# A two-layer mixer kernel with its transposed operands laid block by block

## The chip, the cores and the metric

One core of one Trainium2 chip runs the whole program. The metric is the time of one execution in device microseconds (us); the kernel before was timed three times, and the median counts. The engines are TensorE (PE, with its weight loads PEld), VectorE (DVE), ScalarE (ACT), GpSimd (POOL) and SyncE (SP), which in this kernel issues the DMAs, one after the other from one queue.

## The reference

The input is one sequence of 2048 rows of 1024 numbers in float32. Two layers follow each other. Each layer multiplies its rows by a wide matrix, gives the columns to several mixers, and multiplies the joined results by a second matrix:

```
h = rms_norm(x) ; proj = h @ w_in            # 1024 -> 4652 columns
y = five mixers on the columns of proj       # gating, attention with forgetting, mLSTM, RWKV-7, memory
x1 = x + (y * silu(z)) @ w_out               # 1280 -> 1024
h2 = x1 @ w_in_2                             # 1024 -> 3272 columns
o  = sparse attention (top 256 keys per row) and HGRN-2 on the columns of h2
out = layer_norm(2**0.25 * x1 + o @ w_o_2)   # 1024 -> 1024
```

All of it has to come out with the precision of float32.

## The kernel before

The rows are cut into 16 blocks of 128. Every product with a matrix needs the rows transposed: 128 numbers of the inner dimension on the partitions. A block of 128 rows and 1024 columns is eight such tiles of 128 x 128. For precision each number is split into a high and a low part of type fp32r, and a product is three matmuls (high x high, high x low, low x high), lines 313 to 315 in `mm3`.

The transposed, split rows live in "slots". `split_tiles` makes one tile `slot` of 2 x `k.slot` numbers on each partition, and gives it the shape (part, tile a, row t): first all of the high part, then all of the low part, and in each, for each of the eight tiles a, the rows of all the blocks of that slot one after the other. A slot holds two or three blocks of eight tiles (`k.slot` is 3072 or 2048). So one block in it is 16 pieces of 128 numbers, 512 bytes each, on every partition. Two or three slots are in turn.

A slot is filled in two ways. `put_slots` with `put_T` transposes a block on PE into PSUM, writes the high part with ACT (line 269) and the low part with DVE (line 270), four tiles at a time; where the block is needed again, it stores it with one DMA of 1 MB in DRAM (line 248), in the tensor `xT` (11 blocks of the first layer) or `X1T` (16 blocks of the second). There a block's 16 pieces follow each other: 8 KB in a row for each partition. `get_slots` brings a block back with one DMA of 1 MB (line 255): 11 loads from `xT`, and 32 from `X1T`, where each block is used twice. That makes 27 stores and 43 loads, 70 transfers.

Two functions use slots. In `product_steps` (by way of `project_tm`) a block's tile is the stationary operand and the matrix streams; in the trace such a product reads `pj<-whi,slot`, the moving operand first. In `project_cm` the matrix is stationary and the rows of all two or three blocks of a slot stream at once, 256 or 384 columns: `pj<-slot,whi`. The matrices come by `load_w`: raw pieces (`wraw`, line 297) that ACT and POOL split (lines 300, 301), or, where they were put aside before, both parts ready from DRAM (line 284), 1 to 1.25 MB with 8 to 10 KB in a row on each partition.

The program runs in stages: the first layer's projections with RWKV and the forgetting attention between them (to some 1000 us), its other mixers and projections (to 1700 us), the output product and the second layer's first projections with the choice of keys (`dsa_pick`, to 2490 us and beyond), the second projections for HGRN (`proj2_chunk(..., "hgrn")`, chunks of 6, 6 and 4 blocks, 2493 to 3070 us), the gates (`gates`, 3070 to 3190 us) and the attention with the final product. A planner puts each engine's instructions in order when the program is built; loads of slots and of matrices are asked for early (`high_priority`). SP's queue runs in order, too: a transfer that has to wait holds all the later ones.

Of the kernel before, what the change touches and what calls it, by code (L numbers as in the profile page):

```python
# [9 lines left out]
F32 = mybir.dt.float32  # L10
F32R = mybir.dt.float32r
# [4 lines left out]
ALU = mybir.AluOpType  # L16
# [68 lines left out]
def bc(ap, n=128):  # L85

    return bass.AP(tensor=ap.tensor, offset=ap.offset, ap=[[0, n]] + [list(x) for x in ap.ap])
# [124 lines left out]
def rep(ap, d):  # L212

    s = list(ap.shape)
    return ap.unsqueeze(len(s)).to_broadcast(s + [d])
# [4 lines left out]

def split_tiles(k, nk=8):

    slot = k.big.tile([128, 2, k.slot], F32R, tag="slot", name="slot")
    n = k.slot // nk // 128 * 128
    return slot[:, :, 0:nk * n].rearrange("p q (a t) -> p q a t", a=nk)


def make_slots(k, fill, blocks, nk=8):

    per = k.slot // nk // 128  # L230
    per = -(-len(blocks) // -(-len(blocks) // per))
    slots = []
    for i, b in enumerate(blocks):
        if i % per == 0:
            v = split_tiles(k, nk)
            slots.append((v[:, 0], v[:, 1], min(per, len(blocks) - i)))
        with k.tc.high_priority(k.ahead):
            c = 128 * (i % per)
            fill(v[:, :, :, c:c + 128], b)
    return slots  # L240


def put_slots(k, rows, blocks, nk=8, keep=None):

    def fill(v, b):
        put_T(k, v[:, 0], v[:, 1], 0, rows(b), nk)
        if keep is not None:
            k.nc.sync.dma_start(out=keep[b], in_=v.rearrange("p q a t -> p (q a) t").bitcast(F32))
    return make_slots(k, fill, blocks, nk)


def get_slots(k, kept, blocks):

    def fill(v, b):
        k.nc.sync.dma_start(out=v.rearrange("p q a t -> p (q a) t").bitcast(F32), in_=kept[b])
    return make_slots(k, fill, blocks)


def put_T(k, hi, lo, col, rows, nk):

    nc = k.nc
    for g in range(0, nk, 4):
        n = min(4, nk - g)
        p = k.bank("tp", k.ptp)
        for j in range(n):
            k.transpose(p[:, 128 * j:128 * j + 128], rows[:, (g + j) * 128:(g + j) * 128 + 128])
        pv = p.rearrange("p (a t) -> p a t", a=4)[:, 0:n]
        h = hi[:, g:g + n, col:col + 128]
        nc.scalar.activation(out=h, in_=pv, func=ACT.Copy)
        nc.vector.tensor_tensor(out=lo[:, g:g + n, col:col + 128], in0=pv, in1=h.bitcast(F32), op=ALU.subtract)  # L270


def load_w(k, w, c0, c1, nk, more=(), keep=None):
# [35 lines left out]
def mm3(k, out, pairs, n):  # L309

    m = len(pairs)
    for i, (ah, al, bh, bl) in enumerate(pairs):
        k.nc.tensor.matmul(out=out, lhsT=ah, rhs=bh, start=(i == 0), stop=False)  # L313
        k.nc.tensor.matmul(out=out, lhsT=ah, rhs=bl, start=False, stop=False)  # L314
        k.nc.tensor.matmul(out=out, lhsT=al, rhs=bh, start=False, stop=(i == m - 1))  # L315


def project_steps(k, slots, w, c0, c1, nk, use, more=(), keep=None):

    yield from product_steps(k, slots, *load_w(k, w, c0, c1, nk, more, keep), use)  # L320


def product_steps(k, slots, wh, wl, use):

    nk, n = wh.shape[1:]
    b = 0
    for hi, lo, nb in slots:
        for j in range(nb):
            p = k.bank(k.pj_tag, k.pj)
            t = slice(128 * j, 128 * j + 128)  # L330
            mm3(k, p[:, 0:n], [(hi[:, a, t], lo[:, a, t], wh[:, a, 0:n], wl[:, a, 0:n]) for a in range(nk)], n)
            use(b, p[:, 0:n])
            b += 1
            yield
# [7 lines left out]
def project_cm(k, slots, w, c0, c1, nk, use, more=(), keep=None):  # L342

    wh, wl = load_w(k, w, c0, c1, nk, more, keep)
    for c in range(0, c1 - c0 + sum(b - a for a, b in more), 128):
        m = slice(c, c + 128)
        b = 0
        for hi, lo, nb in slots:
            p = k.bank(k.pj_tag, k.pj)
            t = slice(0, 128 * nb)  # L350
            mm3(k, p[:, t], [(wh[:, a, m], wl[:, a, m], hi[:, a, t], lo[:, a, t]) for a in range(nk)], 128 * nb)
            use(c // 128, b, p[:, t])
            b += nb


def norm_rows(k, x, g, b):

    nc = k.nc
    xt = k.wk.tile([128, D], F32, tag="xt", name="xt", bufs=2)
    nc.sync.dma_start(out=xt, in_=x)  # L360
    sq = k.wk.tile([128, D], BF16, tag="xs", name="xsq", bufs=1)
    ss = k.sm.tile([128, 1], F32, tag="xss", name="xss")
    nc.scalar.activation(out=sq, in_=xt, func=ACT.Square, accum_out=ss)
    nc.vector.tensor_scalar(out=ss, in0=ss, scalar1=1.0 / D, scalar2=EPS, op0=ALU.mult, op1=ALU.add)
    r = k.sm.tile([128, 1], F32, tag="xr", name="xr")
    k.rsqrt(r, ss, "x")
    nc.vector.scalar_tensor_tensor(out=xt, in0=xt, scalar=r[:, 0:1], in1=g, op0=ALU.mult, op1=ALU.mult)
    return xt
# [163 lines left out]
def mem_setup(k, mem, mem_norm_g, w_kv, k_g):  # L532

    nc = k.nc
    g = k.wk.tile([128, D], F32, tag="xt", name="mg")
    nc.sync.dma_start(out=g, in_=bc(mem_norm_g))
    v = split_tiles(k)
    hi, lo = v[:, 0], v[:, 1]
    for b in range(2):
        put_T(k, hi, lo, 128 * b, norm_rows(k, mem[b * 128:b * 128 + 128, :], g, b), 8)  # L540
    k.mem_d = k.dr.tile([64, 4, 256], F32, name="mem_kd"), k.dr.tile([128, 2, 256], F32, name="mem_vd")
    gcol = col2(k, "mgk", k_g, 1.0)
    for c in (0, 256):
        wh, wl = load_w(k, w_kv, c, c + 256, 8)
        for b in range(2):
            t = slice(128 * b, 128 * b + 128)
            p = k.bank("pj", k.pj)
            mm3(k, p[:, 0:256], [(hi[:, a, t], lo[:, a, t], wh[:, a, 0:256], wl[:, a, 0:256]) for a in range(8)], 256)
            x = k.wk.tile([128, WMAX], F32, tag="po", name="mkv", bufs=3)[:, 0:256]
            k.evict(x, p[:, 0:256])  # L550
            if c:
                nc.sync.dma_start(out=k.mem_d[1][:, b], in_=x)
                continue
            hx = x.rearrange("p (h d) -> p h d", d=64)
            sq = k.wk.tile([128, 256], F32, tag="zt", name="msq").rearrange("p (h d) -> p h d", d=64)
            r = k.head_rms(hx, 4, 64, "x", sq=sq)
            nc.vector.tensor_tensor(out=hx, in0=hx, in1=rep(r, 64), op=ALU.mult)
            p = k.bank("tp", k.ptp)
            for h in range(4):
                k.transpose(p[0:64, 128 * h:128 * h + 128], x[:, 64 * h:64 * h + 64])  # L560
            for i in range(2):
                o = k.wk.tile([128, 384], F32, tag="pq", name="mko")[0:64, 0:256]
                nc.vector.tensor_scalar(out=o, in0=p[0:64, 256 * i:256 * i + 256], scalar1=gcol[:, 0:1], scalar2=None,
                                        op0=ALU.mult)
                nc.sync.dma_start(out=k.mem_d[0][:, 2 * i:2 * i + 2, t], in_=o.rearrange("p (h t) -> p h t", h=2))
# [15 lines left out]
def col2(k, name, g, scale):  # L581

    c = k.const.tile([64, 1], F32, name=name)
    k.nc.sync.dma_start(out=c, in_=g.rearrange("(p o) -> p o", o=1))
    if scale != 1.0:
        k.nc.vector.tensor_scalar(out=c, in0=c, scalar1=scale, scalar2=None, op0=ALU.mult)
    return c
# [851 lines left out]
def gates(k, S, slots, wh, wl, blocks):  # L1439

    def use(b, p):
        o = k.wk.tile([128, 392], F32, tag="pg", name="pg")
        silu2(k, o, p, 392)
        k.nc.sync.dma_start(out=S["ga"][128 * blocks[b]:128 * blocks[b] + 128, 120:512], in_=o)

    for _ in product_steps(k, slots, wh, wl, use):
        pass
# [72 lines left out]
def final_attention(k, hold, g, w_o, ln_g, ln_b, out):  # L1520
    w = [load_w(k, w_o[0:512], c, c + 512, 4) for c in (0, 512)]
    for b, x in hold.items():
        v = split_tiles(k, 4)
        hi, lo = v[:, 0], v[:, 1]
        put_T(k, hi, lo, 0, g[b], 4)
        for c, (wh, wl) in zip((0, 512), w):
            p = k.bank("pj", k.pj)
            mm3(k, p, [(hi[:, a, 0:128], lo[:, a, 0:128], wh[:, a], wl[:, a]) for a in range(4)], 512)
            k.nc.vector.tensor_tensor(out=x[:, c:c + 512], in0=x[:, c:c + 512], in1=p, op=ALU.add)
        final_norm(k, x, ln_g, ln_b, out, b)  # L1530

# [776 lines left out]
```

## Time and profile before

| | |
|---|---|
| Median of three runs | 3763.75 us (3760.35 to 3767.74) |
| The profiled execution | 3754.19 us, of which the span of the trace is 3752.3 us |
| Busy: PE / DVE / ACT / POOL | 3521.8 / 2430.2 / 1393.1 / 624.0 us |
| Mean granted clock of PE | 0.962 |
| DMA | 692 MB, mean 185 GB/s |

Busy time is the time in which an engine has an instruction under way. "Idle before" is the time for which the engine stood still ahead of an instruction, with what released it. The granted clock is a share of full speed; 1.00 is TensorE at 2.4 GHz, 0.50 at 1.2 GHz. On the SP queue the length of a DMA row is the time that the issue took, not the transfer; "us to landing" is the time from the issue until the data is there. A row with x2 or more joins several issues that follow each other, with what lay between them.

### The profile page before, as it was taken

How to read it: one execution, taken by the hardware profiler on the slowest of the kernel's cores; microseconds unless marked ns; L12 is line 12 of the kernel's file. 1: busy time of each engine (PE TensorE's matmuls, PEld its weight loads, DVE VectorE, ACT ScalarE, POOL GpSimd, SP SyncE). 2: the span in 40 equal slices, each digit the busy share in tenths (PEclk: the TensorE clock that was granted, in tenths of full speed). 3: DMA queues.
4: the chain of work that ended last, by engine and by line, in shares of the span. 5: the costliest groups of instructions: out<-in, count | busy, mean ns of one | idle time of the engine just before them, and what ended most of it. 6: DMA issues, size and time to landing. Idle time of an engine off the chain costs nothing. (4 is left out here: it accounts for less than half of the span.)

```text
span 3752.3 us, 74094 instructions
## 1 busy us (share of the span) xinstructions
PE 3521.8 (94%) x28365; PEld 3272.7 (87%) x28365; DVE 2430.2 (65%) x7159; ACT 1393.1 (37%) x3007; POOL 624.0 (17%) x582
## 2 busy tenths in 40 slices
PE   6899999999899999899999999989989999899997
PEld 5899999988789999788889899878989988899997
DVE  5477777776644543477674377879976764575675
ACT  3221221222434434444341255557621112444443
POOL 2322222343200000002120000002211112321121
PEclk8999999999899999888899999989999999899999
DMA  8674444454552342437878777776575658453433
GB/s 293 200 220 151 134 154 132 128 183 143 182 191 78 122 163 93 149 124 247 258 262 269 239 242 244 229 214 203 187 235 187 231 181 244 162 201 117 157 110 119
DMA packets 449905, 692.35 MB, mean 185 GB/s; under 512 B 80308, under 2 KB 368510, under 8 KB 410628
## 3 DMA queue, kind: packets, MB, share of 16 engines
q1 hardware_dynamic: 449540, 687.51, 55.7%
q8 instruction: 225, 3.69, 0.4%
q14 instruction: 140, 1.15, 0.1%
HBM read 454.69 MB, written 232.69 MB: 183 GB/s over the span
## 5 line engine op out<-in xcount | busy, mean ns | idle before, releaser
L313 PE MATMUL pj<-whi,slot 128*128 128x256 f32 (+3 forms) x3856 | 1128.4, 293 | 33.9 <-DVE po L177 17.4
L315 PE MATMUL pj<-whi,slot 128*128 128x256 f32 (+3 forms) x3856 | 1120.5, 291 | 2.9 <-DVE slot L270 2.9
L314 PE MATMUL pj<-wlo,slot 128*128 128x256 f32 (+3 forms) x3856 | 1120.3, 291 | 0.8 <-POOL wlo L301 0.8
L313 PEld LDWEIGHTS pj<-whi,slot 128*128 128x128 f32 x3856 | 745.2, 193 | 57.6 <-DVE po L177 18.2
L314 PEld LDWEIGHTS pj<-wlo,slot 128*128 128x128 f32 x3856 | 746.1, 194 | 17.8 <-issue 11.9
L315 PEld LDWEIGHTS pj<-whi,slot 128*128 128x128 f32 x3856 | 744.4, 193 | 18.6 <-issue 9.4
L313 PE MATMUL pj<-slot,whi 128*128 128x256 f32 (+1 forms) x1280 | 383.2, 299 | 27.3 <-DMA slot<-X1T 10.4
L314 PE MATMUL pj<-slot,whi 128*128 128x256 f32 (+1 forms) x1280 | 378.4, 296 | 0.0
L315 PE MATMUL pj<-slot,wlo 128*128 128x256 f32 (+1 forms) x1280 | 377.8, 296 | 0.2 <-POOL wlo L301 0.2
L301 POOL TENSOR_TENSOR wlo<-wraw,whi 128x512 fp32r<-128x512 f32 (+4 forms) x196 | 261.7, 1347 | 640.4 <-ACT whi L300 599.2
L313 PEld LDWEIGHTS pj<-slot,whi 128*128 128x128 f32 x1280 | 250.9, 196 | 38.5 <-issue 16.8
L315 PEld LDWEIGHTS pj<-slot,wlo 128*128 128x128 f32 x1280 | 250.4, 196 | 4.7 <-issue 1.6
L314 PEld LDWEIGHTS pj<-slot,whi 128*128 128x128 f32 x1280 | 250.9, 196 | 3.3 <-issue 1.6
L175 ACT ACTIVATE PT<-tp 128x512 f32<-128x512 f32 (+3 forms) x320 | 162.9, 529 | 239.2 <-PE tp L180 202.7
L1652 ACT ACTIVATE ir<-i 128x512 f32<-128x512 f32 (+2 forms) x304 | 160.1, 543 | 104.9 <-PE i L1650 42.4
L1653 DVE SCALAR_TENSOR_TENSOR sc<-ir,iw,sc 128x512 f32<-128x512 f32 (+2 forms) x266 | 186.4, 701 | 16.6 <-ACT ir L1652 8.3
L1650 PE MATMUL i<-ik,iq 128*128 128x512 f32 (+2 forms) x608 | 170.5, 386 | 21.2 <-ACT ir L1652 17.9
L300 ACT ACTIVATE whi<-wraw 128x512 fp32r<-128x512 f32 (+4 forms) x196 | 117.8, 620 | 191.4 <-DMA wraw<-in_w_in_dram 103.3
L180 PE MATMUL tp<-c_ident,P 128*128 128x128 f32 x1088 | 168.7, 278 | 0.3 <-ACT PT L175 0.2
L1885 PE MATMUL o<-PT,cM 128*128 128x128 f32 x1088 | 143.1, 276 | 1.8 <-ACT PT L175 1.4
L605 DVE TENSOR_SCALAR_CACHE_REDUCE P<-s 128x512 f32<-128x512 f32 (+3 forms) x160 | 94.1, 609 | 77.8 <-PE s L831 65.5
L1753 ACT ACTIVATE dst<-sc,dste 128x256 bf16<-128x256 f32 (+5 forms) x126 | 120.0, 952 | 57.1 <-DVE dste L1720 50.3
(523 smaller groups left out, 6752.5 us busy)
## 6 DMA issues: line engine op xcount, KB each, us to landing
slot<-X1T SPq DMA_DIRECT2D x32, 1024.0 KB, 9.2
wraw<-in_w_in_dram SPq DMA_DIRECT2D x96, 256.0 KB, 3.6
X1T<-slot SPq DMA_DIRECT2D x16, 1024.0 KB, 7.6
xT<-slot SPq DMA_DIRECT2D x11, 1024.0 KB, 6.8
slot<-xT SPq DMA_DIRECT2D x11, 1024.0 KB, 9.2
yr<-Y SPq DMA_DIRECT2D x16, 640.0 KB, 7.2
sD<-po SPq DMA_DIRECT2D x64, 132.0 KB, 3.1
xt<-in_x_dram SPq DMA_DIRECT2D x16, 512.0 KB, 4.7
```

Source lines behind the costliest of these rows:

```text
L175: self.nc.scalar.activation(out=out, in_=in_, func=ACT.Copy)
L180: self.nc.tensor.matmul(out=out, lhsT=in_, rhs=self.ident[0:in_.shape[0], 0:in_.shape[0]], is_transpose=True, start=True, stop=True)
L300: nc.scalar.activation(out=h, in_=raw, func=ACT.Copy)
L301: nc.gpsimd.tensor_tensor(out=lo[:, g:g + m, 0:n], in0=raw, in1=h.bitcast(F32), op=ALU.subtract)
L313: k.nc.tensor.matmul(out=out, lhsT=ah, rhs=bh, start=(i == 0), stop=False)
L314: k.nc.tensor.matmul(out=out, lhsT=ah, rhs=bl, start=False, stop=False)
L315: k.nc.tensor.matmul(out=out, lhsT=al, rhs=bh, start=False, stop=(i == m - 1))
L1650: nc.tensor.matmul(out=p[:, 0:n], lhsT=iq[:, h], rhs=k.ik[:, i, s0:s0 + n], start=(i == 0), stop=(i == 1))
L1652: nc.scalar.activation(out=r, in_=p[:, 0:n], func=ACT.Relu, scale=0.125)
L1653: nc.vector.scalar_tensor_tensor(out=o, in0=r, scalar=k.iw[:, qb, h:h + 1], op0=ALU.mult, op1=ALU.add, in1=o if h else k.dsa_tiny[:, s0:s0 ...
L1753: nc.scalar.activation(out=trash2[:, 0:LA], in_=scs[i][:, L - LA:L], func=ACT.Sign, scale=-1.0, bias=ti, accum_out=ca[:, i:i + 1])
L1885: nc.tensor.matmul(out=o[:, 0:128], lhsT=k.cM[:, j0 + j], rhs=PT[:, 128 * j:128 * j + 128], start=(j0 + j == 0), stop=(j0 + j == ns - 1))
```

## The change

The slot's shape becomes (block b, part q, tile a, row t). A block is then 16 tiles of 128 numbers without a gap, 8 KB in a row on each partition, high part first: the same order as in `xT` and `X1T`. Both sides of the transfers are written as one row of 2048 numbers for each partition. The users are changed to match: `product_steps` and `put_T` take a block's parts, and `project_cm` streams its 256 or 384 columns as two or three runs of 128, which lie 8 KB apart. The slot's size, the number of blocks in it, the number of slots, all loops, matmuls, evictions and DMAs stay as they are.

```diff
 def split_tiles(k, nk=8):
-    slot = k.big.tile([128, 2, k.slot], F32R, tag="slot", name="slot")
-    n = k.slot // nk // 128 * 128
-    return slot[:, :, 0:nk * n].rearrange("p q (a t) -> p q a t", a=nk)
+    slot = k.big.tile([128, 2 * k.slot], F32R, tag="slot", name="slot")
+    n = k.slot // nk // 128
+    return slot[:, 0:n * 256 * nk].rearrange("p (b q a t) -> p b q a t", b=n, q=2, a=nk)
...
-            c = 128 * (i % per)
-            fill(v[:, :, :, c:c + 128], b)
+            fill(v[:, i % per], b)
...
-            k.nc.sync.dma_start(out=keep[b], in_=v.rearrange("p q a t -> p (q a) t").bitcast(F32))
+            k.nc.sync.dma_start(out=keep[b].rearrange("p a t -> p (a t)"), in_=v.rearrange("p q a t -> p (q a t)").bitcast(F32))
...
-        k.nc.sync.dma_start(out=v.rearrange("p q a t -> p (q a) t").bitcast(F32), in_=kept[b])
+        k.nc.sync.dma_start(out=v.rearrange("p q a t -> p (q a t)").bitcast(F32), in_=kept[b].rearrange("p a t -> p (a t)"))
...
-        h = hi[:, g:g + n, col:col + 128]
+        h = hi[:, g:g + n]
         nc.scalar.activation(out=h, in_=pv, func=ACT.Copy)
-        nc.vector.tensor_tensor(out=lo[:, g:g + n, col:col + 128], in0=pv, in1=h.bitcast(F32), op=ALU.subtract)
+        nc.vector.tensor_tensor(out=lo[:, g:g + n], in0=pv, in1=h.bitcast(F32), op=ALU.subtract)
...
-            mm3(k, p[:, 0:n], [(hi[:, a, t], lo[:, a, t], wh[:, a, 0:n], wl[:, a, 0:n]) for a in range(nk)], n)
+            mm3(k, p[:, 0:n], [(v[:, j, 0, a], v[:, j, 1, a], wh[:, a, 0:n], wl[:, a, 0:n]) for a in range(nk)], n)
...
-            p = k.bank(k.pj_tag, k.pj)
-            t = slice(0, 128 * nb)
-            mm3(k, p[:, t], [(wh[:, a, m], wl[:, a, m], hi[:, a, t], lo[:, a, t]) for a in range(nk)], 128 * nb)
+            p = k.bank(k.pj_tag, k.pj)[:, 0:128 * nb]
+            mm3(k, p.rearrange("p (b t) -> p b t", t=128),
+                [(wh[:, a, m], wl[:, a, m], v[:, 0:nb, 0, a], v[:, 0:nb, 1, a]) for a in range(nk)], 128 * nb)
```

`mem_setup` and `final_attention` are changed in the same way.

## Rows read from the trace of the kernel before

**Rows 1.** Profile page, part 1: busy time, share of the span, instructions of each engine.

```profile
PE 3521.8 (94%) x28365; PEld 3272.7 (87%) x28365; DVE 2430.2 (65%) x7159; ACT 1393.1 (37%) x3007; POOL 624.0 (17%) x582
```

**Rows 2.** Who waited for whom, PE: us in total, times, longest us.

```profile
PE pj L313 <- DMA slot<-X1T: 10.4, 2, 6.2
```

**Rows 3.** Timeline, SP queue, 1934 us: start, length, line, transfer (8 to 10 KB pieces).

```profile
1934.08 0.41 SPq L284 DMA_DIRECT2D wlo<-w18l  x1
1934.65 0.36 SPq L1391 DMA_DIRECT2D s2q<-pq  x1
```

**Rows 4.** Timeline, SP queue, 2029 us: a store of a slot, and the next transfer.

```profile
2029.08 0.60 SPq L248 DMA_DIRECT2D X1T<-slot  x1
2029.72 4.76 SPq L1001 DMA_DIRECT2D cog<-sC  x1
```

**Rows 5.** Profile's DMA issues: transfer, count, KB each, median us to landing.

```profile
slot<-X1T SPq DMA_DIRECT2D x32, 1024.0 KB, 9.2
whi<-w19h SPq DMA_DIRECT2D x3, 1280.0 KB, 6.1
```

**Rows 6.** Windows of 25 us: PE, PEld, DVE, ACT, POOL busy; PEclk, DMA share, GB/s.

```profile
2125.00:2150.00 25.00, 20.67 (x167) 19.73 (x166) 5.55 (x15) 4.42 (x9) 1.29 (x1) 0.99 1.03 377
2500.00:2525.00 25.00, 12.27 (x26) 6.53 (x26) 19.88 (x39) 10.23 (x33) 3.20 (x1) 0.52 0.98 274
2725.00:2750.00 25.00, 14.62 (x87) 14.27 (x86) 20.85 (x52) 3.10 (x6) 4.45 (x1) 0.73 0.82 272
3150.00:3175.00 25.00, 23.00 (x128) 22.35 (x126) 4.76 (x15) 2.99 (x6) 2.58 (x2) 1.00 1.01 308
```

**Rows 7.** Timeline, SP queue, 2727 to 2737 us.

```profile
2727.32 5.27 SPq L255 DMA_DIRECT2D slot<-X1T  x2
2732.64 4.32 SPq L284 DMA_DIRECT2D whi<-w29h  x1
```

**Rows 8.** Timeline, PE, 2725 to 2741 us; in brackets idle time before, and its end.

```profile
2729.79 0.55 PE L313 MATMUL pj<-slot,whi 128*128 128x256 f32 x1 [4.19 <-DMA slot<-X1T]
...
2733.90 0.28 PE L314 MATMUL pj<-slot,whi 128*128 128x256 f32 x1
2734.02 0.28 PE L315 MATMUL pj<-slot,wlo 128*128 128x256 f32 x1
2740.49 0.55 PE L313 MATMUL pj<-slot,whi 128*128 128x256 f32 x1 [6.19 <-DMA slot<-X1T]
2740.84 0.41 PE L314 MATMUL pj<-slot,whi 128*128 128x256 f32 x1
2741.05 0.41 PE L315 MATMUL pj<-slot,wlo 128*128 128x256 f32 x1
```

**Rows 9.** Timeline, SP queue, 2499 to 2521 us.

```profile
2499.15 12.24 SPq L255 DMA_DIRECT2D slot<-X1T  x4
...
2518.99 2.19 SPq L297 DMA_DIRECT2D wraw<-in_w_in_dram  x2
```

**Rows 10.** Timeline, PE, 2525 us: the first product of that stage.

```profile
2525.55 0.58 PE L313 MATMUL pj<-slot,whi 128*128 128x256 f32 x1 [1.83 <-ACT whi L300]
```

**Rows 11.** Timeline, SP queue, 3071 us: behind two loads of slots.

```profile
3070.73 3.97 SPq L297 DMA_DIRECT2D wraw<-in_w_in_dram  x1
```

**Rows 12.** Timeline, PE, 3080 us: the first product of the gates.

```profile
3080.35 0.62 PE L313 MATMUL s<-whi,slot 128*128 128x392 f32 x2 [3.11 <-ACT whi L300]
```

**Rows 13.** Groups by line: count, busy us, mean ns, idle before, releasers.

```profile
L313 PE MATMUL pj<-slot,whi 128*128 128x256 f32 (+1 forms) x1280 | 383.2, 299 | 27.3 <-DMA slot<-X1T 10.4
...
L1233 PE MATMUL rb<-rwimg,rwLl 128*128 128x128 f32 x384 | 52.6, 278 | 0.1
L1249 PE MATMUL rb<-rwaZ,rwimg 128*128 128x128 f32 x128 | 16.8, 274 | 0.0
```

**Rows 14.** Groups by line and shape, ACT: a contiguous write, and the slot's.

```profile
L175 ACT ACTIVATE PT<-tp 128x512 f32<-128x512 f32 x224 | 128.5, 594 | 164.6 <-PE tp L180 150.7 <-PE o L624 13.0 <-PE s L833 0.5
L269 ACT ACTIVATE slot<-tp 128x512 fp32r<-128x512 f32 x132 | 75.9, 595 | 110.2 <-PE tp L180 95.8 <-PE pj L315 13.8
```

More of the change, by code (lines that the diff above doesn't have):

```diff
@@ L235, in make_slots @@
             v = split_tiles(k, nk)
-            slots.append((v[:, 0], v[:, 1], min(per, len(blocks) - i)))
+            slots.append((v, min(per, len(blocks) - i)))
         with k.tc.high_priority(k.ahead):
-            c = 128 * (i % per)
-            fill(v[:, :, :, c:c + 128], b)
+            fill(v[:, i % per], b)
     return slots
@@ L245, in fill @@
     def fill(v, b):
-        put_T(k, v[:, 0], v[:, 1], 0, rows(b), nk)
+        put_T(k, v[:, 0], v[:, 1], rows(b), nk)
         if keep is not None:
-            k.nc.sync.dma_start(out=keep[b], in_=v.rearrange("p q a t -> p (q a) t").bitcast(F32))
+            k.nc.sync.dma_start(out=keep[b].rearrange("p a t -> p (a t)"), in_=v.rearrange("p q a t -> p (q a t)").bitcast(F32))
     return make_slots(k, fill, blocks, nk)
@@ L254, in fill, with put_T @@
     def fill(v, b):
-        k.nc.sync.dma_start(out=v.rearrange("p q a t -> p (q a) t").bitcast(F32), in_=kept[b])
+        k.nc.sync.dma_start(out=v.rearrange("p q a t -> p (q a t)").bitcast(F32), in_=kept[b].rearrange("p a t -> p (a t)"))
     return make_slots(k, fill, blocks)
-def put_T(k, hi, lo, col, rows, nk):
+def put_T(k, hi, lo, rows, nk):
     nc = k.nc
@@ L326, in product_steps @@
     b = 0
-    for hi, lo, nb in slots:
+    for v, nb in slots:
         for j in range(nb):
             p = k.bank(k.pj_tag, k.pj)
-            t = slice(128 * j, 128 * j + 128)
-            mm3(k, p[:, 0:n], [(hi[:, a, t], lo[:, a, t], wh[:, a, 0:n], wl[:, a, 0:n]) for a in range(nk)], n)
+            mm3(k, p[:, 0:n], [(v[:, j, 0, a], v[:, j, 1, a], wh[:, a, 0:n], wl[:, a, 0:n]) for a in range(nk)], n)
             use(b, p[:, 0:n])
@@ L347, in project_cm @@
         b = 0
-        for hi, lo, nb in slots:
-            p = k.bank(k.pj_tag, k.pj)
-            t = slice(0, 128 * nb)
-            mm3(k, p[:, t], [(wh[:, a, m], wl[:, a, m], hi[:, a, t], lo[:, a, t]) for a in range(nk)], 128 * nb)
-            use(c // 128, b, p[:, t])
+        for v, nb in slots:
+            p = k.bank(k.pj_tag, k.pj)[:, 0:128 * nb]
+            mm3(k, p.rearrange("p (b t) -> p b t", t=128),
+                [(wh[:, a, m], wl[:, a, m], v[:, 0:nb, 0, a], v[:, 0:nb, 1, a]) for a in range(nk)], 128 * nb)
+            use(c // 128, b, p)
             b += nb
@@ L537, in mem_setup @@
     v = split_tiles(k)
-    hi, lo = v[:, 0], v[:, 1]
     for b in range(2):
-        put_T(k, hi, lo, 128 * b, norm_rows(k, mem[b * 128:b * 128 + 128, :], g, b), 8)
+        put_T(k, v[:, b, 0], v[:, b, 1], norm_rows(k, mem[b * 128:b * 128 + 128, :], g, b), 8)
     k.mem_d = k.dr.tile([64, 4, 256], F32, name="mem_kd"), k.dr.tile([128, 2, 256], F32, name="mem_vd")
@@ L547, in mem_setup @@
             p = k.bank("pj", k.pj)
-            mm3(k, p[:, 0:256], [(hi[:, a, t], lo[:, a, t], wh[:, a, 0:256], wl[:, a, 0:256]) for a in range(8)], 256)
+            mm3(k, p[:, 0:256], [(v[:, b, 0, a], v[:, b, 1, a], wh[:, a, 0:256], wl[:, a, 0:256]) for a in range(8)], 256)
             x = k.wk.tile([128, WMAX], F32, tag="po", name="mkv", bufs=3)[:, 0:256]
@@ L1523, in final_attention @@
         v = split_tiles(k, 4)
-        hi, lo = v[:, 0], v[:, 1]
-        put_T(k, hi, lo, 0, g[b], 4)
+        hi, lo = v[:, 0, 0], v[:, 0, 1]
+        put_T(k, hi, lo, g[b], 4)
         for c, (wh, wl) in zip((0, 512), w):
             p = k.bank("pj", k.pj)
-            mm3(k, p, [(hi[:, a, 0:128], lo[:, a, 0:128], wh[:, a], wl[:, a]) for a in range(4)], 512)
+            mm3(k, p, [(hi[:, a], lo[:, a], wh[:, a], wl[:, a]) for a in range(4)], 512)
             k.nc.vector.tensor_tensor(out=x[:, c:c + 512], in0=x[:, c:c + 512], in1=p, op=ALU.add)
```

## Prediction

> **What bounds the kernel now.** I read the busy times first. PE is busy for 94% of the span and DVE for 65% [rows 1], so the time is PE's work plus what PE waits for; a change that takes nothing from PE's work can only give back some of the 230 us in which PE stands still, and some of what it loses at the lower clock after standing still. The list of waits names the slots' own loads for only 10.4 us [rows 2]. That alone would be a gain of 0.3%. So I looked at the SP queue around these transfers, and there is something larger: a transfer of a slot holds up whatever is issued after it. A store of a slot takes 0.60 us to issue, and the transfer behind it takes 4.76 us [rows 4]; a 1.25 MB load of a ready matrix, which has long rows on both sides, takes 0.41 us, and the one behind it 0.36 us [rows 3]. The list of the queue's waits names no semaphore for such a stall. The transfer with 16 pieces per partition is what differs, so I read it as the queue working off 2048 pieces. There are 70 such transfers.
>
> Then I looked for the windows of 25 us in which PE loses most and a slot's transfer is near. Three stand out: 2725 to 2750 us (14.6 us busy, clock 0.73), 2500 to 2525 us (12.3 us busy, clock 0.52) [rows 6], and the start of the gates at 3080 us [rows 12].
>
> **The change part by part.**
>
> *The issue.* 16 pieces per partition become one. The nearest row for the new form is the ready matrix: 0.41 us to issue, and no stall behind it [rows 3]. So each transfer frees 4.76 - 0.36 = 4.4 us of the SP queue at most; I take 3.5 us, since the stalls behind other slots are 3.97 and 4.32 us [rows 7, 11] and part of a stall may be a wait that stays. Nothing at all would be the lower bound.
>
> *The transfer itself.* A slot's load lands after 9.2 us in the median, the 1.25 MB matrix after 6.1 us [rows 5]. Where the DMA engines are full, the stretch with slots moves 308 GB/s at a share of 1.01, the one with matrices 377 at 1.03 [rows 6]; for each unit of share that is 305 against 366 GB/s, so 1 MB costs 3.4 us before and 2.9 us after. I take a landing after 5.5 us, just under the larger matrix's 6.1 us; the bounds are 5 and 9.2 us.
>
> Here a rule of the Trainium skill speaks against the change. "DMA: Bandwidth & Descriptors", section "Specifications", gives 512 bytes as the smallest transfer for full line rate. By it pieces of 512 bytes have nothing to gain, 1 MB would cost 3.4 us after as before, and the transfer's part of what follows would be gone. The two full stretches speak against it (305 and 366 GB/s), though they carry other transfers as well.
>
> *Site 1, the second HGRN chunk, 2725 us.* PE is through with the first slot's product at 2725.6 us, waits 4.19 us, works on the second's from 2729.79 to 2734.1 us, and waits 6.19 us for the third [rows 8]. The third slot's two loads are issued from 2727.32 us on, in 5.27 us, and the matrix behind them takes another 4.32 us [rows 7]. Now without stalls. A product is 24 matmuls, 2.9 us at one every 0.12 us [rows 8], for a block before as for a slot here; so PE ended the chunk before at 2722.7 us, and its last two blocks began at 2716.9 us. The second slot's buffer is free then, its loads land 5.5 us later at 2722.4 us, and nobody waits for them. The third's is free at 2722.7 us; its loads land at 2728 to 2729 us, and PE is through with the second slot at 2725.6 + 2.9 = 2728.5 us. So 10.4 us shrink to about 0.8: 9.6 us back. Behind each wait PE runs at a matmul every 0.21 us [rows 8], at a lower clock: the second slot's 24 take 4.35 us in place of 2.9, the third's lose 24 x 0.09 = 2.2 us, together 3.7 us. That makes 13.3 us; the bounds are 4 us (only the issue of the last pair is earlier) and 14.1 us.
>
> *Site 2, the first HGRN chunk, 2493 us.* Four loads of slots hold the queue for 12.24 us from 2499.15 us; only at 2518.99 us do the raw matrix pieces go out [rows 9], and the first product starts at 2525.55 us, released by ACT's split of them [rows 10]. With 0.4 us each the queue is through some 14 us earlier. But the six loads of slots stay ahead of these pieces on the DMA engines: 6 x 2.9 = 17.4 us from 2493 us, so the pieces land at about 2511 to 2512 us, and after ACT's other work the product starts at about 2515 us, 10 us earlier. Some of the time thus freed PE had used for the scores of the key choice, which must still be done beside it; in 10 us of that window they are 10 x 12.3/25 x 0.52 = 2.6 us at full clock [rows 6]. I take 8 us; the bounds are 0 (DVE is busy for 19.9 of 25 us in that window [rows 6], and could become what PE waits for) and 13.
>
> *Site 3, the gates, 3070 us.* Behind two loads of slots the first raw piece takes 3.97 us to issue [rows 11]; PE waits 3.11 us for its split at 3080.35 us [rows 12]. The stall goes, and the wait with it: I take 3.5 us with the lower clock behind it, between 0 and 5.
>
> *The other transfers.* Some 54 of the 70 stand in stretches where PE is busy nearly throughout. 54 x 3.5 us = 189 us of queue; PE stands still for 6% of the span [rows 1], and if that share of the stalls is what it waits for, 11 us. Much of it is hidden behind DVE's chains, so I take 4 us, between 0 and 11.
>
> *Edits at nothing.* ACT's writes into the slot become contiguous; the contiguous write of the same size takes 594 ns, the slot's 595 ns [rows 14], so there is nothing to gain or lose, and DVE's write is of the same kind. The stationary tile is 128 numbers in a row before and after. No wait is added, and buffers and their sizes stay.
>
> *The moving operand in runs.* The products of `project_cm` are 3 x 1280 = 3840 matmuls [rows 13]; each now streams two or three runs 8 KB apart. The nearest row is L1249, whose moving operand is two runs of 64: 16.8 us / 128 = 131 ns each, against 52.6 / 384 = 137 ns for L1233, one run of 128 [rows 13]. So I take 0. It is float32 and not fp32r, so a cost can't be excluded; the rival below prices it. A gain has no reason, as the columns are the same.
>
> The sum: 13.3 + 8 + 3.5 + 4 = 29 us. Against the profiled execution's own 3754.19 us (its span of 3752.3 us and 1.9 us around it, which nothing here touches) that is 3725 us. The median of the runs lies 9.6 us above this execution; I take the 29 us off the median: 3763.75 - 29 = 3735 us. What is late next at the sites is DVE's work on the key choice (site 2), PE itself (site 1) and DVE's HGRN chain (site 3).
>
> **The rivals.**
>
> *The stalls were hidden.* The queue's stalls lie beside PE's work except at site 1, and the time won there is spent again in the next wait for DVE. For it: at site 2 DVE is busy for four fifths of the window, more than PE [rows 6]. Against it: PE's waits at site 1 name the slots themselves [rows 2]. By the line-rate rule above, this is where it would end. About 4 us gained: 3760 us.
>
> *More comes back.* All bounds at their good end: 14.1 + 13 + 5 + 11 = 43 us, 3720 us. For it: every stall delays loads, and PE's lower clock behind each wait makes it dearer. Against it: most of the span has PE full.
>
> *Runs cost on PE: slower.* If each further run makes PE start its stream anew, 3840 matmuls pay at least once. As an estimate: a 256-column product comes every 120 ns, of which 256 columns at 2.4 GHz are 107, which leaves 13 ns for a start. 3840 x 13 = 50 us, less the 29 us: 3785 us. The change would lose from 29 / 3840 = 7.5 ns for each matmul on. For it: no row shows fp32r in runs. Against it: L1249. A new order of the planner, which would set the same work in another sequence, could cost a few us as well; its size can't be had from the trace, and its chance is in this case.
>
> **How the numbers follow.** The forecast has a chance of 0.50, more back 0.18, hidden 0.18, slower 0.14. A measurement of this kernel tells 0.2%, 7.5 us, from no change. The forecast and "more" are faster by over that: 0.68; "hidden" is the same: 0.18; slower: 0.14. The range has to hold 8 in 10: from 3710 us (all good ends and a little more from the clock) to 3775 us, which takes in the hidden case and a cost for the runs that outweighs part of the gain, and leaves out most of the slower case and a tail of "more". The forecast alone would be 3722 to 3750 us.
>
> **What would show it.** Right: transfers behind a slot's issue in 0.3 to 0.5 us; a slot's load landing after 5 to 6 us; the waits for `slot<-X1T` on PE down from 10.4 to about 1 us; the first HGRN product some 10 us earlier against the end of the stage before; the matmuls `pj<-slot,whi` with the same means as now. Wrong: stalls of some 4 us that stay behind contiguous transfers, which would mean that the bytes make them and not the pieces; means of `pj<-slot,whi` that rise by 8 ns or more; PE waits for DVE that grow by what the slots' waits lost.

## The result and the profile after

The changed kernel takes 3725.59 us in the median of six runs (3721.09 to 3741.80), the kernel before 3759.27 us in six runs beside it: a ratio of 0.9927, 95% interval 0.9908 to 0.9945, or 27 us of 3759 (the two medians lie 34 us apart; a second set of runs, below, gives 0.9929 and 27 us). The prediction was 3735 us with a range of 3710 to 3775, and "faster" with a chance of 0.68.

The profiled execution is the slowest of the six: 3741.80 us, a span of 3740.0. It lies only 12 us below the profiled execution of before, so this trace shows less of the gain than the median. The profiled execution of that second set, `again`, has a span of 3736.4 us.

The profile's parts 1 and 2 of the changed kernel (busy time, share, instructions; the packets of all DMAs):

```profile
PE 3526.1 (94%) x28365; PEld 3277.3 (88%) x28365; DVE 2425.2 (65%) x7159; ACT 1391.6 (37%) x3007; POOL 623.1 (17%) x582
...
DMA packets 398065, 692.35 MB, mean 185 GB/s; under 512 B 80308, under 2 KB 313214, under 8 KB 355332
```

The engines' busy times are within 5 us of what they were [rows 1], and the bytes are the same (692 MB). The instructions stand in the same order on every engine in both programs, so nothing here comes from a new schedule.

The SP queue's timeline where [rows 4] and [rows 7] stood (start, length, line, transfer; line numbers are up to two lower now):

```profile
2028.63 0.48 SPq L248 DMA_DIRECT2D X1T<-slot  x1
2029.16 0.63 SPq L999 DMA_DIRECT2D cog<-sC  x1
...
2714.20 0.84 SPq L255 DMA_DIRECT2D slot<-X1T  x2
2715.14 5.32 SPq L1369 DMA_DIRECT2D s2gb<-po  x2
2720.55 0.40 SPq L284 DMA_DIRECT2D wlo<-w29l  x1
2721.04 0.90 SPq L255 DMA_DIRECT2D slot<-X1T  x2
2721.98 0.68 SPq L284 DMA_DIRECT2D whi<-w29h  x1
```

The transfer behind a store is issued in 0.63 us and not in 4.76, a pair of slot loads in 0.90 and not in 5.27, the matrix behind it in 0.68 and not in 4.32. These stalls went as predicted; others stay, as the experiments show. The landings did less than predicted; the profile's DMA issues (transfer, count, KB each, median us to landing):

```profile
slot<-X1T SPq DMA_DIRECT2D x32, 1024.0 KB, 7.3
...
xT<-slot SPq DMA_DIRECT2D x11, 1024.0 KB, 5.7
slot<-xT SPq DMA_DIRECT2D x11, 1024.0 KB, 7.5
```

A slot's load lands after 7.3 us: less than the 9.2 of [rows 5], not the 5.5 I had taken. And the list of waits of PE (us in total, times, longest) still holds

```profile
PE pj L313 <- DMA slot<-X1T: 6.4, 2, 4.2
```

where [rows 2] had 10.4 and the prediction about 1. The two sites in the timeline of PE, with idle time before and its end in brackets (before: [rows 8, 10]):

```profile
2521.75 0.39 PE L313 MATMUL pj<-slot,whi 128*128 128x256 f32 x1 [1.42 <-ACT whi L300]
...
2725.01 0.55 PE L313 MATMUL pj<-slot,whi 128*128 128x256 f32 x1 [2.20 <-DMA slot<-X1T]
...
2733.76 0.56 PE L313 MATMUL pj<-slot,whi 128*128 128x256 f32 x1 [4.16 <-DMA slot<-X1T]
```

Both waits at site 1 shrank by 2 us each; neither went away.

**Where the time came from.** Each column below is one execution. Two executions drift against each other by as much as 15 us in stretches that have little to do with the change (the profiled one of after loses that much between 525 and 950 us, `again` doesn't). So I matched the DVE rows of each trace in their order with those of before, took the difference of the starts, and kept what recurs. In us, change of this difference (its median per 50 us) around the place, negative is time gained:

| place (time in before) | after | again | loads8k | pad2k | pad1k | stores8k | pad512 |
|---|---|---|---|---|---|---|---|
| 0 to 300 us (stores of `xT`) | -4.3 | -5.8 | -1.8 | -4.6 | +0.3 | -4.9 | -0.1 |
| 1050 us (loads of `xT`) | -3.1 | -3.1 | -2.9 | -3.3 | -1.6 | -1.7 | 0.0 |
| site 2, 2500 us | -5.8 | -5.8 | -5.8 | -5.8 | -4.9 | -0.1 | -0.5 |
| site 1, 2750 us | -4.0 | -4.3 | -4.7 | -4.4 | -3.2 | -0.5 | -1.0 |
| site 3, 3100 us | -1.7 | -4.6 | -4.0 | -5.3 | -3.2 | -0.8 | -1.7 |

The right columns are the experiments. The three sites give 11.5 to 14.7 us, the loads of `xT` at 1050 us another 3, the first 300 us some 5. Steps of 1 to 2 us prove little here: at site 3 `pad512`, which has 512-byte pieces, shows the same -1.7 as the first trace of the changed kernel.

### The profile page after: what moved, and what is told of

It reads as the page before. It is cut to its first block, busy times and chain, and to the rows that moved or that the text cites. A ratio compares the mean times of both kernels' runs of the same rounds, so it can differ in the third digit from the quotient of the medians.

```text
span 3740.0 us, 74097 instructions
## 1 busy us (share of the span) xinstructions
PE 3526.1 (94%) x28365; PEld 3277.3 (88%) x28365; DVE 2425.2 (65%) x7159; ACT 1391.6 (37%) x3007; POOL 623.1 (17%) x582
## 3 DMA queue, kind: packets, MB, share of 16 engines
q14 instruction: 140, 1.15, 0.1%
## 5 line engine op out<-in xcount | busy, mean ns | idle before, releaser
L1648 PE MATMUL i<-ik,iq 128*128 128x512 f32 (+2 forms) x608 | 169.4, 385 | 14.7 <-ACT ir L1650 12.1
```

The source lines that it names most:

```text
L1648: nc.tensor.matmul(out=p[:, 0:n], lhsT=iq[:, h], rhs=k.ik[:, i, s0:s0 + n], start=(i == 0), stop=(i == 1))
```

## The experiments

Theory Q was the prediction's: 2048 pieces of 512 bytes keep the SP queue busy, and what stands behind them comes late. Its first rivals: the new slot layout helps the compute engines (L), or the stores alone carry the gain (S). A further one, E, came out of the first four runs: the DMA engines are full at the sites and pass fewer bytes per us in short pieces.

### The level, and the layout without the long pieces

`again` is the changed kernel itself. `pad512` keeps its slot layout and spreads the DRAM side:

```diff
-xT, X1T = (k.dr.tile([NB, 128, 16, 128], ...
+xT, X1T = (k.dr.tile([NB, 128, 16, 144], ...
...
-out=keep[b].rearrange("p a t -> p (a t)"), in_=v...
+out=keep[b][:, :, 0:128], in_=v... "p (m t) -> p m t", m=16
```

(the loads likewise)

> The changed kernel once more, unchanged, so that its trace can be read beside those of its variants. Theory Q (a 1 MB transfer in 2048 pieces of 512 bytes keeps SP's queue from issuing the next one for 3.5 to 5 us, and weight or slot loads behind it arrive late): 0.990 to 0.995 of the kernel before, SP's next issue after a pair of slot loads within 1 us, waits of the products for slot<-X1T some 6 us in all. Theory L (the gain is in the slots' new layout on the compute engines, not in the transfers): the same time; this run doesn't tell the two apart, it is the level for the others.

> The changed kernel with its new slot layout, but each block's 8 KB per partition lies in DRAM as 16 rows of 512 bytes with 64 unused bytes behind each, so that all 70 transfers go in 512-byte pieces on both sides. Theory Q: the gain is gone: 3750 to 3765 us, 0.997 to 1.002 of the kernel before; pairs of slot loads hold SP for 3.5 to 5 us again, and the waits for slot<-X1T are back at about 10 us. Theory L: the layout is all there, so 3720 to 3735 us, 0.991 to 0.994.

`again`: 3731.06 us, 0.9929 (0.9914 to 0.9944). `pad512`: 3761.67 us, 1.0009 (0.9994 to 1.0024). With the layout alone nothing is left: L is out. The stalls are back (SP queue of `pad512`):

```profile
2734.16 3.65 SPq L255 DMA_DIRECT2D slot<-X1T  x2
2741.87 0.40 SPq L284 DMA_DIRECT2D wlo<-w29l  x1
2742.36 5.27 SPq L255 DMA_DIRECT2D slot<-X1T  x2
```

### Stores alone, loads alone

`stores8k` gives the slots that are loaded the layout of before, `loads8k` those that are stored:

```diff
-def split_tiles(k, nk=8):
+def split_tiles(k, nk=8, apart=False):
+    if apart:
+        return slot... "p q (a b t) -> p b q a t"
...
```

> Only the 27 stores go in one piece per partition; the 43 loads write a slot in the layout of the kernel before, 16 pieces of 512 bytes per partition. Theory Q puts most of the gain on the loads (sites at 2500, 2727 and 3062 us, where no store is near): 3748 to 3756 us, 0.997 to 0.999 of before, with the holds of 3.5 to 5 us behind the pairs of loads still there. Rival S (the gain comes with the packets that fell, and in the profile only the stores' packets fell, by 27 x 1920): 3722 to 3732 us, 0.990 to 0.994, as the whole change.

> Only the 43 loads go in one piece per partition; the 27 stores are made from slots in the layout of the kernel before, 16 pieces of 512 bytes per partition. Theory Q: most of the gain stays, 3728 to 3742 us, 0.992 to 0.996 of before; a store holds SP for 4 to 5 us again at the matrix loads near 2029 us, the loads no longer do. Rival S: no gain, 3750 to 3765 us, 0.998 to 1.002.

`stores8k`: 3753.58 us, 0.9995 (0.9980 to 1.0009). `loads8k`: 3737.86 us, 0.9953 (0.9939 to 0.9966). The loads carry 0.47% alone, some 18 us of 27; the stores alone are at most 0.2%, though between `loads8k` and the whole change there are another 0.24%. In the table `stores8k` has no step at a site. S falls, and it was a misreading of the profile. The count of packets of `loads8k`:

```profile
DMA packets 449905, 692.35 MB, mean 186 GB/s; under 512 B 80308, under 2 KB 368510, under 8 KB 410628
```

That is the count of before to the packet, at a gain of 18 us. In the whole change it had fallen by 51,840 = 27 x 1920, the 27 stores alone. In `stores8k`, whose 43 loads write 16 pieces per partition, it is the changed kernel's, 398,065. So for these loads the count doesn't show pieces on the side that is written. In `pad512`, where the DRAM side is in pieces, it is 532,465, and 134,400 = 70 x 1920 above the changed kernel: there the 27 stores count in pieces too, though the slot that they read lies without a gap. What the count follows in a store is therefore not shown.

### Larger pieces: 1 KB and 2 KB

As `pad512`, with 8 rows of 1 KB or 4 of 2 KB in DRAM. By then I had seen that the sites have full DMA engines, and E was on the table:

> The changed kernel with each block's 8 KB per partition in four pieces of 2 KB (64 unused bytes behind each in DRAM), in stores and loads. Theory E (the DMA engines are full at the sites, and each piece costs them a fixed time on top of its bytes; full stretches near 2500 us move about 298 GB/s in 512-byte pieces and 422 in 8 KB pieces at a share of 1.02, so about 9 ns a piece and 19 ns per 512 bytes): about 380 GB/s there, four fifths of the gain, 0.993 to 0.996 of the kernel before. Theory Q (the queue is held by the number of pieces; a quarter of the pieces, a quarter of the hold): about the same time, but with holds of 1 us behind a pair and no rise of the bytes per us at full share. A rival (anything under 8 KB is no use, or all above 512 bytes is enough): 0.999 to 1.001, or 0.9925 to 0.9935.

> The same in eight pieces of 1 KB. Theory E: about 345 GB/s in the full stretches, half of the gain, 0.995 to 0.998 of the kernel before. Theory Q: half the hold, 2 us behind a pair, half the gain. If 512 bytes alone were the trouble, the whole gain, 0.992 to 0.994.

`pad2k`: 3736.18 us, 0.9939 (0.9922 to 0.9956). `pad1k`: 3743.45 us, 0.9957 (0.9941 to 0.9974). With 0.9929 for 8 KB and 1.0009 for 512 bytes the gain follows the size of the pieces, as both theories wanted. The windows tell more. Eight us from 2 us after the first slot load of site 2 on, the same work in each (PE, PEld, DVE, ACT, POOL busy; clock, DMA share, GB/s). Before, 512 bytes:

```profile
2495.00:2503.00 8.00, 5.18 (x16) 2.69 (x16) 7.76 (x22) 6.84 (x16) 0.97 (x1) 0.87 0.99 299
```

`pad1k`:

```profile
2504.25:2512.25 8.00, 5.56 (x16) 2.89 (x16) 7.76 (x22) 6.85 (x16) 0.97 (x1) 0.82 1.09 357
```

`pad2k`:

```profile
2493.95:2501.95 8.00, 5.19 (x16) 2.70 (x16) 7.76 (x22) 6.83 (x16) 0.97 (x1) 0.86 1.04 389
```

`again`, 8 KB:

```profile
2493.15:2501.15 8.00, 5.20 (x16) 2.70 (x16) 7.76 (x22) 6.83 (x16) 0.98 (x1) 0.88 1.01 413
```

The DMA share is about 1 in all four, and they pass 299, 357, 389 and 413 GB/s; E had said 345 and 380 for the two in the middle, Q no rise at all. The same stretch gives 299 GB/s in `stores8k`, and 409 in `after` and in `loads8k`. And the holds don't vanish with the pieces: in `pad2k` a pair still takes 1.33 to 2.13 us to issue, and in the changed kernel itself, behind six slot loads (SP queue):

```profile
2496.38 2.23 SPq L255 DMA_DIRECT2D slot<-X1T  x4
2498.65 1.83 SPq L1455 DMA_DIRECT2D lbl<-in_lb_logits_dram  x2
2502.63 7.60 SPq L166 DMA_DIRECT2D kv_g<-in_kv_norm_g_dram  x1
2510.27 4.43 SPq L1612 DMA_DIRECT2D cM<-s2cw  x4
2514.86 0.90 SPq L297 DMA_DIRECT2D wraw<-in_w_in_dram  x2
```

So a hold reads better as what stands in front not having drained yet; short pieces drain more slowly. Nothing here shows how much a queue takes before it holds.

The Trainium skill's "DMA: Bandwidth & Descriptors", section "Why small descriptors are slow (HBM only)", gives each packet a fixed cost of about 3 cycles beside one cycle for 32 bytes. As an estimate from that page, 512 bytes would take 16 + 3 cycles and 8 KB 256 + 3: 8 KB would be 1.17 times as fast. The trace has 413 / 299 = 1.38 (1.35 for each unit of share), so the direction agrees and the size doesn't. The rule of the Trainium skill weighed in the prediction, that 512 bytes are enough for the full rate, does not hold here, as the 299 GB/s show.

### Short pieces with a free SP queue

Here Q and E part. `bh_p` is the kernel before with the HGRN chunks' slot loads issued by POOL; `ah_p` is the changed kernel with the same edit (`get_slots` passes the engine on to its `dma_start`).

```diff
-proj2_chunk(k, S2, get_slots(k, X1T, blocks), ..., "hgrn")
+proj2_chunk(k, S2, get_slots(k, X1T, blocks, nc.gpsimd), ..., "hgrn")
```

> The kernel before, 512-byte pieces everywhere, but the 16 slot loads of the HGRN chunks (sites 1 and 2) are issued from POOL's queue and not from SP's, so that SP can't be held by them. From 2490 us on some instructions stand in another order than before. Theory Q (SP's held queue is what costs): the steps of these two sites, 5.8 and 4.3 us in the changed kernel, come here too without the longer pieces, some 10 us, 0.996 to 0.998 of the kernel before. Theory E (the full engines and the bytes they pass are what costs): SP's queue is free, yet the full stretches still move 290 to 320 GB/s, and the two steps don't come, 0.999 to 1.002.

> The changed kernel, 8 KB pieces everywhere, with the 16 slot loads of the HGRN chunks issued from POOL's queue: the pair to bh_p, which is the same with 512-byte pieces, and whose instructions stand in the same order but for some matmuls at site 2. In neither can these loads hold SP. Theory E (full engines pass more bytes in long pieces): the whole gain is there between the two, about 27 us, 0.996 to 0.998 of the kernel before against 1.0043 for bh_p; at site 1 the waits for the second and third slot, 5.50 and 5.56 us in bh_p, fall to 2 to 4 us, and the full stretch there moves 400 GB/s in place of 334. Theory Q (SP's held queue): nothing is left for the change to give at sites 1 and 2, so some 17 us between the two, 0.9995 to 1.001, and the two waits at site 1 stay at about 5.5 us.

`bh_p`: 3776.47 us, 1.0043 (1.0024 to 1.0063). `ah_p`: 3756.56 us, 0.9996 (0.9981 to 1.0011). In both many instructions from 2500 us on stand in another order, and PE's waits for the evicted scores (`ir`), 17.9 us in total before and 12.1 after, grow to 34.3 and 29.5 us, so neither is to be read against before. Between the two are 0.47%, 18 us; they differ in order from each other too. The 18 us and the total of `ah_p` are what was written down for Q (the total of `bh_p` was in neither's range); with intervals of 0.2% to either side E's 27 us lie at the edge. The totals don't settle it. Site 1 tells the two apart. SP's timeline in `bh_p` there, the ready matrices behind the last slot loads:

```profile
2737.59 0.38 SPq L284 DMA_DIRECT2D wlo<-w29l  x1
2738.07 0.39 SPq L284 DMA_DIRECT2D whi<-w29h  x1
```

PE, where the first of the three rows is the first slot's product:

```profile
2738.09 0.35 PE L313 MATMUL pj<-slot,whi 128*128 128x256 f32 x1 [1.08 <-DMA slot<-X1T]
...
2746.69 0.55 PE L313 MATMUL pj<-slot,whi 128*128 128x256 f32 x1 [5.50 <-DMA slot<-X1T]
...
2757.71 0.55 PE L313 MATMUL pj<-slot,whi 128*128 128x256 f32 x1 [5.56 <-DMA slot<-X1T]
```

SP is held by nothing, and PE waits as long as ever. The same rows of `ah_p`, where the first slot's product starts at 2737.07 us:

```profile
2742.53 0.35 PE L313 MATMUL pj<-slot,whi 128*128 128x256 f32 x1 [2.42 <-DVE dste L1754]
...
2750.75 0.55 PE L313 MATMUL pj<-slot,whi 128*128 128x256 f32 x1 [3.62 <-DVE rs_t L195]
```

The products read neither `dste` nor `rs_t`. The trace's times to landing tell what they waited for (`slot` in `ah_p`, 2735 to 2752 us):

```profile
DMA to landing us min/median/max: 8.2/10.4/12.6
```

The later of the third slot's two loads was issued at 2738.05 us and landed 12.6 us later, at 2750.6, just ahead of the product. For every kernel but `wlo8`, which follows, counted from the start of the first slot's product:

| | issue of the third slot's two loads begins | third slot's product |
|---|---|---|
| before, pad512, stores8k (512 B) | +4.8, +4.7, +5.1 us | +17.9, +17.5, +18.2 |
| bh_p (512 B, SP free) | -0.7 | +19.6 |
| pad1k, pad2k | +1.1, +1.2 | +14.8, +14.4 |
| after, again, loads8k, kvact (8 KB) | +1.3, +0.7, +1.0, +1.0 | +14.0, +14.0, +13.2, +14.6 |
| ah_p (8 KB, SP free) | +0.5 | +13.7 |

An early issue with short pieces gains nothing (19.6); with long pieces it is 13.7. The third slot's loads share the DMA engines there with the two ready matrices, in both runs, and the windows show what these engines passed; `bh_p`:

```profile
2738.00:2754.00 16.00, 8.56 (x48) 8.13 (x48) 12.15 (x41) 8.50 (x15) 6.22 (x3) 0.79 1.02 355
```

`ah_p`:

```profile
2738.00:2750.00 12.00, 6.71 (x42) 6.33 (x40) 9.92 (x28) 5.82 (x10) 5.08 (x3) 0.86 1.02 420
```

That is E at site 1. Pieces that cost time in the queue which feeds the engines, SP's or POOL's alike, would give the same two starts; the DMA share of 1.02 in both windows speaks for the engines. For site 2, site 3, the stores and the rest no run separates E from Q; that the same holds there is carried over, not shown. The same page of the Trainium skill says in "Issuing engines are not separate DMA queues" that transfers run on the same 16 DMA engines whichever engine started them. Site 1 agrees: 17.9 and 19.6 us with short pieces issued by SP and by POOL, 14.0 and 13.7 with long ones.

### The bytes in front of the third slot

Why does PE still wait at site 1? `wlo8` leaves out seven eighths of the low part of one ready matrix, the transfer just ahead of the third slot's loads:

```diff
-for x, d in zip((hi, lo), k.kept[key]):
-    nc.sync.dma_start(out=x.bitcast(F32), in_=d)
+for x, d, m in zip((hi, lo), k.kept[key], (1, 8 if first else 1)):
+    e = nk * n // m
+    nc.sync.dma_start(out=x[:, 0:e].bitcast(F32), in_=d[:, 0:e])
...
```

> The changed kernel with 0.875 MB fewer bytes in front of the third slot's loads at site 1: of the ready matrix w29l only the first eighth is loaded (128 KB), and the products that use it take that eighth for all eight blocks of rows, so the low part of this one matrix is wrong. If what is left of the wait for the third slot (4.1 us in the changed kernel) is bytes at full DMA engines, 0.875 MB at 405 GB/s are 2.3 us: the wait falls to about 1.9 us. If it is the place of the loads in SP's queue behind the stores s2gb, or the slot's buffer that comes free late, the wait stays at about 4 us.

One execution, with a span of 3734.7 us. The third slot's loads are issued from 2720.03 us on, and the first slot's product starts at 2719.52; PE behind it:

```profile
2724.60 0.36 PE L317 MATMUL pj<-slot,whi 128*128 128x256 f32 x1 [2.04 <-DMA slot<-X1T]
...
2731.24 0.55 PE L317 MATMUL pj<-slot,whi 128*128 128x256 f32 x1 [3.54 <-DMA slot<-X1T]
```

The wait fell to 3.54 us only, not to 1.9. But the product starts 11.7 us after the first slot's and not 14.0, 2.3 us earlier, as the bytes said (1.5 to 2.9 earlier against the four kernels with 8 KB in the table). PE worked through the second slot in 3.1 us here and in 4.6 in the changed kernel, and so waited from earlier on. The start goes with the bytes in front, the length of the wait also with PE's pace: in `pad2k`, where PE was as fast, it is 5.94 us with the product at +14.4. This is one execution; I take it as support, no more.

### What holds the queue at site 2

`kvact` moves two of the transfers ahead of `wraw` to ScalarE's queue:

```diff
-    k.kv_g = k.row(kv_g, 128, "kv_g")
+    k.kv_g = k.row(kv_g, 128, "kv_g", k.nc.scalar)
-    nc.sync.dma_start(out=cm, in_=slab(...))
+    nc.scalar.dma_start(out=cm, in_=slab(...))
```

> The changed kernel with the load of kv_g and the four loads of cM issued from ScalarE's queue, so that at site 2 the raw matrix pieces (wraw) stand right behind the slot loads and lbl in SP's queue; in the trace of the changed kernel kv_g and cM hold SP for 7.60 and 4.43 us ahead of them. Theory E: these holds are the six slot loads still being worked off, so wraw goes out once the engines have room, 5 us earlier than with kv_g and cM ahead of it; first HGRN product 3 to 6 us earlier against the stage before, 0.991 to 0.993 of the kernel before. Theory Q (the small loads themselves hold the queue for 12 us): first product some 10 us earlier, 0.989 to 0.991. If DVE, busy for 19 of 20 us there, is what PE waits for: 0.9925 to 0.994, no gain on the changed kernel.

3746.91 us, 0.9966 (0.9953 to 0.9978): 0.4% slower than the changed kernel, which none of the three expected. From site 2 on many instructions of PE, DVE and ACT also stand in another order than in the changed kernel. ScalarE's timeline:

```profile
2502.51 4.61 ACTq L1612 DMA_DIRECT2D cM<-s2cw  x1
2507.17 1.04 ACT L1751 ACTIVATE dst<-sc,dste 128x896 bf16<-128x896 f32 x1 [5.51 <-issue]
```

The hold moved with the transfers to an engine whose work PE waits for: PE stands still for 6.38 us, up to 2508.73 us, until ScalarE has evicted its scores, and site 2's step of -5.3 us (2500 and 2550 together) is gone. SP gained little: its last four slot loads now take 12.48 us together and not 2.23. That is no hold. Each of the four issues takes 0.32 to 0.67 us, and between them SP waits (its waits from 2498 to 2511 us):

```profile
SPq L255 <- DMA slot<-X1T: 5.7, 1, 5.7
SPq L255 <- DMA cM<-s2cw: 4.9, 1, 4.9
```

In this trace an issue waits until the earlier transfer that signals on the same semaphore has landed, and in `kvact` the last two slot loads stood behind a slot load and a load of `cM`. In the changed kernel such waits are 1.0 us ahead of the second `lbl` and 2.1 ahead of `kv_g`, beside the holds. `wraw` went out 17.7 us after the first slot load in place of 19.8. For the size of what could be had at site 2 the run says nothing.

## Why the prediction was right, point by point

- **The stall as the place to look: right. Its cause: wrong.** I read it as the queue working off 2048 pieces. `bh_p` shows that freeing SP alone doesn't help at site 1; there the engines' rate decides, which at a share near 1 is 299 GB/s in 512-byte pieces and 413 in long ones (site 2). That the stall is the queue waiting for these engines is the reading that fits best, not more. Over the whole trace, the issues on SP that take more than 1 us add up to 375 us before and 166 after: 209 us went, of 70 x 3.5 = 245 priced. In `stores8k` they are 305, 70 us fewer than before, and next to no time came back. The term for the engines' rate was in the prediction, with 305 and 366 GB/s for each unit of share from [rows 6]: the right mechanism, too small.
- **"Landing after 5.5 us": failed.** 7.3 us in the median; and from the issue of the third slot's loads to its product 12.7 us in after (2721.04 to 2733.76), 13.2 in before (2727.32 to 2740.49). Issued earlier, the loads stand behind more bytes that are still under way, which `wlo8` supports.
- **Site 1, 13.3 us: mis-sized, 4.0 to 4.3 measured.** It is the lower bound named there, only the issue of the last pair being earlier. The waits fell from 10.4 to 6.4 us and not to 0.8, and with waits left, the slow start behind them stayed too, 0.55 and 0.56 us for the first matmul behind each, as in [rows 8].
- **Site 2, 8 us: mis-sized, 5.3 to 5.8.** The raw pieces went out 20 us after the first slot load, where before it was 26 and the prediction had 14 us less; `lbl`, `kv_g` and `cM` took the queue in the meantime, which the prediction hadn't priced. The first product came 26.7 us after the first slot load (2495.06 to 2521.75) and not 32.6 (2493.00 to 2525.55): 5.9 us earlier, where the forecast had 10.
- **Site 3, 3.5 us: inside its bounds, the size open.** -4.6 in `again`, -1.7 in the first trace, and as much in `pad512`. The stall of 3.97 us in the issue of the raw piece is gone, 0.42 us in its place, and PE's wait of 3.11 us for the split is 1.22.
- **The other transfers, 4 us: mis-sized.** 27 less the sites' 14 leaves some 13 us: 3 at 1050 us, about 5 in the first 300 us, and the rest in no place that recurs. These 13 us are a remainder, the difference of medians less steps of single traces, and no run measures them; at their ends the traces of `after` and `again` are 13.7 and 17.2 us ahead of the one before, not 27.
- **Runs cost nothing on PE: right.** The group by line: 300 ns against 299 [rows 13].

```profile
L313 PE MATMUL pj<-slot,whi 128*128 128x256 f32 (+1 forms) x1280 | 383.7, 300 | 21.2 <-DVE phl L1378 6.6
```

- **Edits at nothing: right.** `pad512`, with all of them and 512-byte pieces, is at 1.0009.

So the sum of 29 us was good by luck in part, because two errors met: the sites were put 10 us or more too high (24.8 against 11.5 to 14.7), the rest about as much too low. Of the rivals, "more comes back" (3720 us) is about as near as the forecast by the first six runs, though its sizes for the sites are further off; "hidden" falls with a gain of 27 us in place of 4, and "runs cost on PE" with the 300 ns and with `pad512`.

## What to carry to other kernels

When transfers stall the queue behind them, look at the DMA share and the GB/s of that stretch first. At a share of 1 moving the issue to another engine didn't help here: in `bh_p` SP was free and the third slot came no earlier, in `kvact` the hold went to ScalarE. Longer pieces of the same bytes did help. Price such a change by the bytes that stand in front of the transfer which the busiest engine waits for, at the rate of the new form, and not by the landing of a lone transfer. 2 KB pieces gave most of the gain here (0.9939 against 0.9929). And read a joined row of a queue by its single issues before calling it a stall: it can hold waits.

## What the runs showed of the hardware

- At a DMA share of 0.99 to 1.09, 1 MB loads move 299, 357, 389 and 413 GB/s in pieces of 512 bytes, 1, 2 and 8 KB (site 2, 8 us of one trace each).
- The profile's count of packets doesn't show pieces on the written side of a load: 43 loads went from 16 pieces per partition to one, with 18 us gained, and the count stayed at 449,905 (`loads8k`).
- Slot loads issued by POOL and not by SP take 1.15 us each with 16 pieces per partition and 0.53 us with one, at site 1 in `bh_p` and `ah_p`.
- A load's issue can wait for the landing of an earlier transfer: 5.7 and 4.9 us at site 2 in `kvact`.
